# Features at two distances from the weights, modulo 256 bytes, in a decoder trunk of fp32r products

## The chip, the core and the metric

The kernel runs on one core of a Trainium2 chip. The metric is the device time of the whole program in microseconds, the lower the better. An engine has its own instruction stream: TensorE (PE, with its weight loads shown as PEld), VectorE (DVE), ScalarE (ACT), GpSimd (POOL) and SyncE (SP), which issues the transfers. [...]

## The reference: two macaron layers

The program computes two layers on x of 512 positions by 1024 channels. Each layer is a feed-forward, a mixer and a second feed-forward:

```python
def swiglu(h, w_gate, w_up, w_down):
    return (jax.nn.silu(h @ w_gate) * (h @ w_up)) @ w_down
...
    for l in range(DEPTH):
        x = x + 0.5 * swiglu(rms_norm(x, ffn1_norm[l]), ffn1_w_gate[l], ffn1_w_up[l], ffn1_w_down[l])

        h = rms_norm(x, mix_norm[l])
        a, g, q, k, v = jnp.split(h @ w_in[l], splits, axis=-1)
...
        x = x + jnp.concatenate([conv_out, diff_out], axis=-1) @ w_out[l]

        x = x + 0.5 * swiglu(rms_norm(x, ffn2_norm[l]), ffn2_w_gate[l], ffn2_w_up[l], ffn2_w_down[l])
```

The feed-forward is 2816 wide, 22 tiles of 128. The mixer has a causal convolution and a differential attention side by side.

## The kernel before

**Layout.** Channels lie on the 128 partitions, positions along the free axis, so x is 8 tiles of 128x512 and all of it stays in the on-chip memory. The weights stream in by SyncE's transfers into `wraw`.

**Products by two parts.** Every fp32 operand is split into a high part in fp32r and the rest, also in fp32r: ScalarE copies to `whi`, VectorE subtracts to `wlo` (`parts_of`, lines 105 to 112; `Unit.hi` and `Unit.lo`, lines 387 to 396). A product is then three matmuls, high by high, high weights by low features, low weights by high features (`mm3`, lines 144 to 150; `Unit.product`, lines 405 to 411). The first operand of a matmul is loaded into the array (the weights, 128x128, recorded as a weight load of its own), the second moves through it (the features, 512 or 256 columns). In the projections to q, k and v (lines 988 to 990 and 1018 to 1020) the roles are swapped: a 128x128 piece of features is loaded and 512 columns of weights move.

**A feed-forward** (`ffn`, from line 800) does its 22 tiles in three parts (`PARTS`, line 45). The first 5 are plain: full-width products of 512 columns on `acts` (the scaled x, lines 146, 149, 150), then 480 matmuls in all four feed-forwards for their down product (`ps_d`, on the features `hh` and `hl`). The other 17 tiles, in groups of 8 and 9, go by a Strassen-like scheme of seven products on halves: one `Unit` is one tile's gate and up (`GateUp`) or two output tiles' down products (`Down`), and each of its seven products is four steps of three matmuls 256 columns wide, all at line 409: 84 matmuls. `Unit.body` writes the order of a unit out by hand: while PE does one unit, ScalarE and VectorE split the next one's weights, and GpSimd adds its sums of weights (lines 381 to 385). A feed-forward has 17 `GateUp` and 8 `Down`, in this order: one unit of the first group, its other seven, one of the second, the four `Down` of the first, the other eight, the four `Down` of the second. The ninth tile of the second group is done in full-width products on `sixes` (`plain`, line 640).

**Where the operands of line 409 come from.** `Halves` (line 322) makes what `GateUp` reads: the normalised features, written back over `acts` by `settle` (b11, b21, t1, b22 in `get`), and their sums in `sixes` (t2, t3, t4). `Gated` (line 691) makes what `Down` reads: the gated features in `hh` and `hl` and their sums in tiles named `hs`, for which `part` (line 707) finds twelve places a group, most in the feed-forward's own memory, some in tiles that are free at that time (`rb`, `ssum`, `sq`, `ones_r`, the last tile of `acts`).

**Memory.** Tiles come from pools that are laid one behind the other in the order of lines 79 to 84: const, small, rp (the raw weights), act (x, acts, rb), wp (whi, wlo and their short kinds), tmp (ssum, two sq). A pool opened later (the feed-forward's, the mixer's) lies behind them. Inside a pool tiles lie in the order of their first use. The class `Room` (line 224) makes the feed-forward's memory of a few large blocks: `sixes` of 12 tiles, h0 of 10 and h1 of 12, h3 and h2 of two each, every one `LINE` = 32 elements (128 bytes) longer than its content, which starts `OFF` = 16 elements (64 bytes) in. `acts` has the same form. A block that serves a second purpose is renewed as a whole (`renew`).

Of the kernel before, what the change touches and what calls it, by code (L numbers as in the profile page):

```python
# [18 lines left out]
P = 128  # L19
# [28 lines left out]

SPACE = 408
GAP = 6  # L50
OFF = 16
LINE = 32
SQ = 16
WRAW = 1040
# [19 lines left out]
def trunk(ctx: ExitStack, tc: tile.TileContext, xt, par, lamv, relb, onehot,  # L74
# [24 lines left out]
    def ring(tag, n=1024):  # L99
        if tag == "wraw":  # L100
            return rp.tile([P, WRAW], F32, tag=tag, name=tag, bufs=RING[tag])
        dt = F32 if "raw" in tag else F32R
        return wp.tile([P, n], dt, tag=tag, name=tag, bufs=RING[tag])

# [119 lines left out]
    class Room:  # L224

        def __init__(self, pool):
            self.tile = pool.tile
            self.sixes = self.tile([P, 12 * SEQ + LINE], F32R, tag="sixes", name="sixes")
            names = [[f"{t}{n}" for n in ns for t in ("hh", "hl")] for ns in (range(5), (5, 6), (7,), (8,))]
            names[1] += [f"s{n}" for n in range(5)] + ["ht"]  # L230
            self.where = {name: (k, n) for k, group in enumerate(names) for n, name in enumerate(group)}
            self.blocks = [self.block("h0", 10), self.block("h1", 12, F32), None, None]

        def block(self, tag, n, dtype=F32R):
            return self.tile([P, n * SEQ + LINE], dtype, tag=tag, name=tag)[:, OFF : OFF + n * SEQ]

        def renew(self, k, dtype):
            self.blocks[k] = self.block(f"h{k}", (10, 12, 2, 2)[k], dtype)

        def feat(self, tag):  # L240
            k, n = self.where[tag]
            return self.blocks[k][:, n * SEQ : (n + (3 if tag == "ht" else 1)) * SEQ]

    class Prep:


        def __init__(self, l, gain):
            self.l, self.gain = l, gain
            self.hi, self.lo = acth, actl
            self.s = tmp.tile([P, SEQ], F32, tag="ssum", name="ssum", bufs=1)  # L250

# [9 lines left out]
        def squares(self, k, pin=False):  # L261
            sq = self.s if k == 0 else tmp.tile([P, SEQ + SQ], F32, tag="sq", name="sq")[:, GAP : GAP + SEQ]
# [59 lines left out]
    class Halves:  # L322
# [3 lines left out]

        def __init__(self, fp, pr, r):
            t = fp.sixes[:, OFF : OFF + 12 * SEQ].rearrange("p (i n j c) -> p i n j c", i=2, n=3, j=KT // 2)
            self.th, self.tl = t[:, 0], t[:, 1]

            self.whole = []
            a, b = slice(0, HS), slice(HS, SEQ)
            ht = fp.blocks[1][:, 8 * SEQ : 11 * SEQ].rearrange("p (i n c) -> p i n c", i=2, n=3)
            for j in range(KT // 2):
                for k in (j, j + KT // 2):
                    h = fp.blocks[1][:, len(self.whole) * SEQ : (len(self.whole) + 1) * SEQ]
                    V.scalar_tensor_tensor(h, x[:, k, :], col(pr.l, pr.gain, k), r, op0=ALU.mult, op1=ALU.mult)
                    self.whole.append((k, h))
# [9 lines left out]
        def settle(self):  # L348

            for k, h in self.whole:  # L350
                S.activation(acth[:, k, :], h, AF.Copy)
                V.tensor_tensor(actl[:, k, :], h, f32(acth[:, k, :]), op=ALU.subtract)

        def get(self, name):
            if name[0] == "t" and name != "t1":
                n = int(name[1]) - 2
                return lambda j: (self.th[:, n, j, :], self.tl[:, n, j, :])
            k0, c = {"b11": (0, 0), "t1": (0, HS), "b21": (KT // 2, 0), "b22": (KT // 2, HS)}[name]
            return lambda j: (acth[:, k0 + j, c : c + HS], actl[:, k0 + j, c : c + HS])

# [197 lines left out]
    class Down(Unit):  # L558
# [121 lines left out]
        def rest(self):  # L680
# [8 lines left out]
            self.after(B)  # L689

    class Gated:

        def __init__(self, fp, pairs, many, ahead=False):
            self.fp, self.pairs, self.many, self.ahead = fp, pairs, many, ahead
# [5 lines left out]
        def hold(self, n):  # L700
            if self.ahead and not n:
                return const.tile([P, P + SPACE], F32, tag="ones_r", name="hold")[:, :SEQ]
            if n == (2 if self.ahead else 0):
                self.fp.renew(2 if self.ahead else 3, F32)
            return self.fp.feat(("hh", "hl")[n // 2 % 2] + ("7" if self.ahead else "8"))

        def part(self):

            if not self.slots:
                ht, off = self.fp.feat("ht"), slice(OFF, OFF + SEQ)  # L710
                self.slots = [lambda n=n: ht[:, n * SEQ : (n + 1) * SEQ] for n in range(3)]
                self.slots.append(lambda: act.tile([P, SEQ + LINE], F32R, tag="rb", name="hs")[:, off])
                self.slots += [lambda n=n: self.fp.feat(f"s{n}") for n in range(5)]
                if not self.ahead:
                    self.slots.append(lambda: tmp.tile([P, SEQ], F32R, tag="ssum", name="hs", bufs=1))
                    self.slots += [lambda: tmp.tile([P, SEQ + SQ], F32R, tag="sq", name="hs")[:, off]] * 2
                if self.ahead:
                    self.slots += [
                        lambda: acth[:, KT - 1, :], lambda: actl[:, KT - 1, :],
                        lambda: const.tile([P, P + SPACE], F32R, tag="ones_r", name="hs")[:, off],  # L720
                    ]
            return self.slots.pop(0)()

        def part_ninth(self):

            self.nine = hi, lo = [self.fp.sixes[:, 2 * n * SEQ : 2 * (n + 1) * SEQ] for n in range(2)]
# [30 lines left out]
        def part_hi(self, n, us):  # L757
            if self.spot(n) > 6:
                self.fp.renew(self.spot(n) - 5, F32R)
            hi, lo = (self.fp.feat(f"{t}{self.spot(n)}") for t in ("hh", "hl"))  # L760
            pinned(S.activation(hi, us, AF.Copy))
# [37 lines left out]

    def ffn(pr, gu, dn, after, turn, lead=None, aside=None):  # L800
        with tc.tile_pool(name="ffn", bufs=1) as pool:
            fp = Room(pool)
            r = halves = None
            held, h = [], Gated(fp, 0, PLAIN)
            for m in range(PLAIN):
# [29 lines left out]
                if not halves:  # L835
                    halves = Halves(fp, pr, r)
# [17 lines left out]
            for m0, many, pairs in PARTS[1:]:  # L854
                end = m0 + many == FT
                h = Gated(fp, pairs, many, end)
                gates = [GateUp(fp, halves, gu[m0 + n, 0], gu[m0 + n, 1], n, h) for n in range(many)]
# [392 lines left out]
    for l in range(DEPTH):  # L1250
# [11 lines left out]

        turn = ffn(pr, gu1[l], dn1[l], then(l, "mix_norm"), 2, *((lead, aside) if l == 0 else ()))
        mixer(l, nxt["p"], then(l, "ffn2_norm"), turn)
        ffn(nxt["p"], gu2[l], dn2[l], then(l + 1, "ffn1_norm") if l + 1 < DEPTH else last, 0)
        pr = nxt["p"]
# [74 lines left out]
```

## Time and profile before

| | us |
|---|---|
| median of 3 runs | 1747.37 |
| lowest and highest run | 1746.35, 1750.32 |
| the profiled execution | 1747.69 |
| its span, from the first instruction to the last | 1745.9 |
| PE busy | 1736.4 |
| DVE busy | 1399.3 |
| ACT busy | 1000.0 |
| POOL busy | 891.5 |

A row of the page's groups reads: line, engine, operation, written tile and read tiles, shapes, count, busy us, mean ns of one, and after a second bar the idle time of the engine before them. A matmul's own duration there includes the time in which the next one already runs; from one start to the next is what it costs. A row of the timeline reads: start us, length us, engine, line, operation, tiles, shapes and count. A row of windows reads: the stretch, its length, and for each engine busy us and the count of instructions, then the granted clock, the share of the DMA engines and GB/s.

### The profile page before, as it was taken

The page shows a single profiled execution, that of the slowest core. Times are in us where ns is not written, and L with a number is a line of the kernel's source. Part 1 is how long each engine was busy: PE and PEld are TensorE (multiplying, and loading weights), DVE is VectorE, ACT ScalarE, POOL GpSimd, SP SyncE. Part 2 cuts the span into 40 slices and gives each one's busy share as a digit, 9 for nine tenths or more (in the row PEclk, how much of TensorE's full clock was granted, in tenths as well). Part 3 has the DMA queues.
Part 4 walks back from the last instruction along what each step waited for, and adds up shares of the span by engine and source line. Part 5 has one row for each costly group of instructions (what it writes and reads, how often), then busy time and mean ns, then how long its engine had stood idle before and what let it go on. Part 6 is the DMA issues. An engine that isn't in the chain of part 4 may idle for free.

```text
span 1745.9 us, 30798 instructions
## 1 busy us (share of the span) xinstructions
PE 1736.4 (99%) x12013; PEld 1601.2 (92%) x12013; DVE 1399.3 (80%) x2049; ACT 1000.0 (57%) x1607; POOL 891.5 (51%) x664
## 2 busy tenths in 40 slices
PE   9999999999999999999999999999999999999998
PEld 7899999988788899999988999999887888999998
DVE  6978888868867868888968788888788588788886
ACT  6456566655844456556634665665558354565663
POOL 3165655468753145555503555554787432455552
PEclk9999999999999999999999999999999999999999
DMA  6233333423022233333432333334230232333332
GB/s 229 91 121 100 110 108 103 165 73 104 29 85 85 74 108 102 108 106 109 133 97 73 100 107 110 114 104 145 84 109 25 73 107 75 99 108 109 110 97 86
DMA packets 82932, 177.91 MB, mean 102 GB/s; under 512 B 8952, under 2 KB 30727, under 8 KB 82785
## 3 DMA queue, kind: packets, MB, share of 16 engines
q1 hardware_dynamic: 81184, 174.10, 31.3%
q8 instruction: 94, 1.54, 0.4%
q0 software_dynamic: 1312, 1.67, 0.3%
q14 instruction: 54, 0.43, 0.1%
q10 hardware_dynamic: 288, 0.16, 0.0%
HBM read 173.79 MB, written 3.42 MB: 101 GB/s over the span
## 4 chain that ended last, share of the span: by engine, by line
PE 97%; DVE 2%; ACT 1%; issue 0%; DMA 0%; POOL 0%; DVEq 0%; ACTq 0%; SPq 0%
PE ps_pair L409 55%; PE ps_pair L146 6%; PE ps_pair L149 6%; PE ps_pair L150 6%; PE ps_d L146 2%; PE ps_d L149 2%; PE ps_d L150 2%; PE ps_sc L1112 2%; PE ps_pair L989 2%; PE ps_out L149 2%; PE ps_pair L990 2%; PE ps_pair L988 2%; PE ps_out L150 2%; PE ps_out L146 2%; PE ps_o L1142 1%; PE ps_v L1018 1%
## 5 line engine op out<-in xcount | busy, mean ns | idle before, releaser
L396 DVE TENSOR_TENSOR wlo<-wraw,whi 128x1024 fp32r<-128x1024 f32 (+1 forms) x400 | 497.7, 1252 | 136.5 <-ACT whi L392 133.3
L392 ACT ACTIVATE whi<-wraw 128x1024 fp32r<-128x1024 f32 (+1 forms) x400 | 377.5, 953 | 255.9 <-PE ps_pair L409 116.9
L382 POOL TENSOR_TENSOR wraw<-wraw 128x512 f32<-128x512 f32 x100 | 120.8, 1208 | 585.7 <-DVE wlo L396 281.9
L409 PE MATMUL ps_pair<-acts,whi 128*128 128x256 f32 x2240 | 403.2, 280 | 0.0
L409 PEld LDWEIGHTS ps_pair<-acts,whi 128*128 128x128 f32 x2240 | 342.1, 188 | 0.3
L409 PE MATMUL ps_pair<-acts,wlo 128*128 128x256 f32 x1120 | 312.8, 279 | 0.0
L409 PE MATMUL ps_pair<-sixes,whi 128*128 128x256 f32 x1632 | 291.0, 279 | 0.0
L409 PE MATMUL ps_pair<-h,whi 128*128 128x256 f32 x1536 | 282.0, 280 | 0.3 <-ACT keep L459 0.3
L409 PEld LDWEIGHTS ps_pair<-sixes,whi 128*128 128x128 f32 x1632 | 248.0, 188 | 0.0
L409 PEld LDWEIGHTS ps_pair<-h,whi 128*128 128x128 f32 x1536 | 238.5, 188 | 3.4 <-ACT keep L459 1.0
L409 PE MATMUL ps_pair<-sixes,wlo 128*128 128x256 f32 x816 | 227.7, 279 | 0.0
L109 ACT ACTIVATE whi<-wraw 128x1024 fp32r<-128x1024 f32 (+3 forms) x124 | 123.5, 1002 | 154.4 <-PE ps_pair L149 83.2
L409 PEld LDWEIGHTS ps_pair<-acts,wlo 128*128 128x128 f32 x1120 | 210.2, 188 | 0.0
L409 PE MATMUL ps_pair<-h,wlo 128*128 128x256 f32 x736 | 205.6, 279 | 0.0
L149 PE MATMUL ps_pair<-acts,whi 128*128 128x512 f32 x448 | 175.4, 392 | 0.0
L150 PE MATMUL ps_pair<-acts,wlo 128*128 128x512 f32 x448 | 175.0, 392 | 0.0
L146 PE MATMUL ps_pair<-acts,whi 128*128 128x512 f32 x448 | 174.3, 395 | 0.0
L385 POOL TENSOR_TENSOR wraw<-wraw 128x512 f32<-128x512 f32 x100 | 152.9, 1529 | 7.8
L384 POOL TENSOR_TENSOR wraw<-wraw 128x512 f32<-128x512 f32 x100 | 151.5, 1515 | 7.8
L409 PEld LDWEIGHTS ps_pair<-sixes,wlo 128*128 128x128 f32 x816 | 155.0, 190 | 0.0
L383 POOL TENSOR_TENSOR wraw<-wraw 128x512 f32<-128x512 f32 x100 | 147.1, 1471 | 7.6
L409 PEld LDWEIGHTS ps_pair<-h,wlo 128*128 128x128 f32 x736 | 138.8, 189 | 0.0
(218 smaller groups left out, 3422.5 us busy)
## 6 DMA issues: line engine op xcount, KB each, us to landing
wraw<-in_gu SPq DMA_DIRECT2D x172, 512.0 KB, 3.9
wraw<-in_wqkv SPq DMA_DIRECT2D x24, 512.0 KB, 3.8
wraw<-in_wag SPq DMA_DIRECT2D x16, 512.0 KB, 3.7
wraw<-in_wout SPq DMA_DIRECT2D x16, 512.0 KB, 3.7
wraw<-in_dn SPq DMA_DIRECT2D x60, 128.0 KB, 3.1
wraw<-in_dn SPq DMA_DIRECT2D x20, 384.0 KB, 3.2
wraw<-in_dn SPq DMA_DIRECT2D x28, 256.0 KB, 3.0
wraw<-in_dn SPq DMA_DIRECT2D x20, 320.0 KB, 3.3
```

Source lines behind the costliest of these rows:

```text
L109: S.activation(hi, raw, AF.Copy)
L146: first = T.matmul(ps, wh, xh, start=start, stop=False)
L149: T.matmul(ps, wh, xl, start=False, stop=False)
L150: T.matmul(ps, wl, xh, start=False, stop=stop)
L382: G.tensor_tensor(d, g1, u1, op=ALU.add)
L383: G.tensor_tensor(u1, u2, u1, op=ALU.add)
L384: G.tensor_tensor(m0, g1, u1, op=ALU.add)
L385: G.tensor_tensor(m1, g2, m0, op=ALU.add)
L392: pinned(S.activation(hi, raw, AF.Copy), pin)
L396: pinned(V.tensor_tensor(out=lo, in0=raw, in1=f32(hi), op=ALU.subtract), pin)
L409: mm = T.matmul(ps, l, r, start=first and i == n == 0, stop=False, skip_group_check=True)
L988: T.matmul(ps[n], xh[:, t], wh, start=k == 0, stop=False)
```

## The change

No instruction is added or taken away; the tiles lie at other addresses. The weights' pool comes behind tmp. The two halves of `acts` are padded by `MOST` = 64 elements each, and `split(by)` gives views of them that start `by` elements in: full-width products read `split(0)`, while `settle` writes and `GateUp` reads `split(48)`, 192 bytes further on. The feed-forward's pool begins with a tile `off` of 48 elements, so that all its tiles lie 192 bytes further. `Room` goes: each feature is a tile of its own name again, without padding. `ssum` gets 48 elements of padding, `sq` 8 in place of 16, `ones_r` 392 in place of 408, `rb` none.

```diff
-SPACE = 408
+SPACE = 392
 GAP = 6
-OFF = 16
-LINE = 32
-SQ = 16
+NEAR, FAR = 48, 0
+MOST, SHIFT = 64, (48, 48, 48, 48)
...
+    tmp = ctx.enter_context(tc.tile_pool(name="tmp", bufs=2))
     wp = ctx.enter_context(tc.tile_pool(name="wp", bufs=1))
-    tmp = ctx.enter_context(tc.tile_pool(name="tmp", bufs=2))
...
-    acts = act.tile([P, 2 * KT * SEQ + LINE], F32R, tag="acts", name="acts")[:, OFF : OFF + 2 * KT * SEQ]
-    acts = acts.rearrange("p (n k c) -> p n k c", n=2, k=KT)
-    acth, actl = acts[:, 0], acts[:, 1]
+    acts = act.tile([P, 2, KT * SEQ + MOST], F32R, tag="acts", name="acts")
+
+    def split(by):
+        return [acts[:, n, by : by + KT * SEQ].rearrange("p (k c) -> p k c", k=KT) for n in range(2)]
+
+    acth, actl = split(0)
...
-        r = act.tile([P, SEQ + LINE], F32, tag=tag, name=tag)[:, :SEQ]
+        r = act.tile([P, SEQ], F32, tag=tag, name=tag)
...
-            self.s = tmp.tile([P, SEQ], F32, tag="ssum", name="ssum", bufs=1)
+            self.s = tmp.tile([P, SEQ + NEAR], F32, tag="ssum", name="ssum", bufs=1)[:, :SEQ]
...
-        def __init__(self, fp, pr, r):
-            t = fp.sixes[:, OFF : OFF + 12 * SEQ].rearrange("p (i n j c) -> p i n j c", i=2, n=3, j=KT // 2)
-            self.th, self.tl = t[:, 0], t[:, 1]
+        def __init__(self, fp, pr, r, by):
+            self.hi, self.lo = split(by)
+            self.th = fp.tile([P, 3, KT // 2, HS], F32R, tag="th", name="th")
+            self.tl = fp.tile([P, 3, KT // 2, HS], F32R, tag="tl", name="tl")
...
-                S.activation(acth[:, k, :], h, AF.Copy)
-                V.tensor_tensor(actl[:, k, :], h, f32(acth[:, k, :]), op=ALU.subtract)
+                S.activation(self.hi[:, k, :], h, AF.Copy)
+                V.tensor_tensor(self.lo[:, k, :], h, f32(self.hi[:, k, :]), op=ALU.subtract)
...
         def plain(self, n, us):
-            hi, lo = self.fp.feat(f"hh{n}"), self.fp.feat(f"hl{n}")
+            hi = self.fp.tile([P, SEQ], F32R, tag=f"hh{n}", name="hh")
+            lo = self.fp.tile([P, SEQ], F32R, tag=f"hl{n}", name="hl")
...
-    def ffn(pr, gu, dn, after, turn, lead=None, aside=None):
-        with tc.tile_pool(name="ffn", bufs=1) as pool:
-            fp = Room(pool)
+    def ffn(pr, gu, dn, after, turn, by, lead=None, aside=None):
+        with tc.tile_pool(name="ffn", bufs=1) as fp:
+            if by:
+                fp.tile([P, by], F32, tag="off", name="off")
...
             halves.settle()
-            fp.renew(1, F32R)
```

The last part of `Gated` changes in the same manner: `hold`, `part`, `part_ninth` and `part_hi` take tiles by their names.

More of the change, by code (lines that the diff above doesn't have):

```diff
@@ L102, in ring @@
         dt = F32 if "raw" in tag else F32R
-        return wp.tile([P, n], dt, tag=tag, name=tag, bufs=RING[tag])
+        more = FAR if "raw" in tag else 0
+        return wp.tile([P, n + more], dt, tag=tag, name=tag, bufs=RING[tag])[:, :n]
     def parts_of(raw, hi, lo, eng=None, first=False, pin=False):
@@ L219, in spread @@
                 tc.keep_in_program_order(mm)
-        r = act.tile([P, SEQ + LINE], F32, tag=tag, name=tag)[:, :SEQ]
+        r = act.tile([P, SEQ], F32, tag=tag, name=tag)
         S.activation(r, ps, AF.Copy)
         return r
[L224 to L242, printed above, removed]
     class Prep:
@@ L261, in squares @@
         def squares(self, k, pin=False):
-            sq = self.s if k == 0 else tmp.tile([P, SEQ + SQ], F32, tag="sq", name="sq")[:, GAP : GAP + SEQ]
+            sq = self.s if k == 0 else tmp.tile([P, SEQ + 8], F32, tag="sq", name="sq")[:, GAP : GAP + SEQ]
             square = S.activation(sq, x[:, k, :], AF.Square)
@@ L322, in trunk @@
     class Halves:
-        def __init__(self, fp, pr, r):
-            t = fp.sixes[:, OFF : OFF + 12 * SEQ].rearrange("p (i n j c) -> p i n j c", i=2, n=3, j=KT // 2)
-            self.th, self.tl = t[:, 0], t[:, 1]
+        def __init__(self, fp, pr, r, by):
+            self.hi, self.lo = split(by)
+            self.th = fp.tile([P, 3, KT // 2, HS], F32R, tag="th", name="th")
+            self.tl = fp.tile([P, 3, KT // 2, HS], F32R, tag="tl", name="tl")
             self.whole = []
+            free = [f"{t}{n}" for t in ("hh", "hl") for n in range(5, 9)]
             a, b = slice(0, HS), slice(HS, SEQ)
-            ht = fp.blocks[1][:, 8 * SEQ : 11 * SEQ].rearrange("p (i n c) -> p i n c", i=2, n=3)
+            ht = fp.tile([P, 2, 3, HS], F32, tag="ht", name="ht")
             for j in range(KT // 2):
                 for k in (j, j + KT // 2):
-                    h = fp.blocks[1][:, len(self.whole) * SEQ : (len(self.whole) + 1) * SEQ]
+                    h = fp.tile([P, SEQ], F32, tag=free.pop(), name="hn")
                     V.scalar_tensor_tensor(h, x[:, k, :], col(pr.l, pr.gain, k), r, op0=ALU.mult, op1=ALU.mult)
@@ L689, in rest, with one_tile, __init__ @@
             self.after(B)
+    def one_tile(pool, tag, dtype, name, bufs=None):
+        return pool.tile([P, SEQ], dtype, tag=tag, name=name, **({"bufs": bufs} if bufs else {}))
     class Gated:
-        def __init__(self, fp, pairs, many, ahead=False):
+        def __init__(self, fp, pairs, many, by, ahead=False):
+            self.by = by
             self.fp, self.pairs, self.many, self.ahead = fp, pairs, many, ahead
@@ L702, in hold @@
                 return const.tile([P, P + SPACE], F32, tag="ones_r", name="hold")[:, :SEQ]
-            if n == (2 if self.ahead else 0):
-                self.fp.renew(2 if self.ahead else 3, F32)
-            return self.fp.feat(("hh", "hl")[n // 2 % 2] + ("7" if self.ahead else "8"))
+            return one_tile(self.fp, ("hh", "hl")[n // 2 % 2] + ("7" if self.ahead else "8"), F32, "hold")
         def part(self):
             if not self.slots:
[L710 to L713, printed above, removed]
+                ht = self.fp.tile([P, 3, SEQ], F32R, tag="ht", name="hs")
+                self.slots = [lambda n=n: ht[:, n] for n in range(3)]
+                tags = [(act, "rb", None)] + [(self.fp, f"s{n}", None) for n in range(5)]
                 if not self.ahead:
-                    self.slots.append(lambda: tmp.tile([P, SEQ], F32R, tag="ssum", name="hs", bufs=1))
-                    self.slots += [lambda: tmp.tile([P, SEQ + SQ], F32R, tag="sq", name="hs")[:, off]] * 2
+                    tags += [(tmp, "ssum", 1), (tmp, "sq", None), (tmp, "sq", None)]
+                self.slots += [
+                    lambda pool=pool, tag=tag, bufs=bufs: one_tile(pool, tag, F32R, "hs", bufs)
+                    for pool, tag, bufs in tags
+                ]
                 if self.ahead:
                     self.slots += [
-                        lambda: acth[:, KT - 1, :], lambda: actl[:, KT - 1, :],
-                        lambda: const.tile([P, P + SPACE], F32R, tag="ones_r", name="hs")[:, off],
+                        *(lambda t=t: t[:, KT - 1, :] for t in split(self.by)),
+                        lambda: const.tile([P, P + SPACE], F32R, tag="ones_r", name="hs")[:, :SEQ],
                     ]
@@ L724, in part_ninth @@
         def part_ninth(self):
-            self.nine = hi, lo = [self.fp.sixes[:, 2 * n * SEQ : 2 * (n + 1) * SEQ] for n in range(2)]
+            th = self.fp.tile([P, 6, SEQ], F32R, tag="th", name="nine")
+            self.nine = hi, lo = [th[:, 2 * n : 2 * n + 2, :].rearrange("p n c -> p (n c)") for n in range(2)]
             S.activation(hi, self.ninth, AF.Copy)
@@ L757, in part_hi @@
         def part_hi(self, n, us):
-            if self.spot(n) > 6:
-                self.fp.renew(self.spot(n) - 5, F32R)
-            hi, lo = (self.fp.feat(f"{t}{self.spot(n)}") for t in ("hh", "hl"))
+            hi = one_tile(self.fp, f"hh{self.spot(n)}", F32R, "hh")
+            lo = one_tile(self.fp, f"hl{self.spot(n)}", F32R, "hl")
             pinned(S.activation(hi, us, AF.Copy))
@@ L835, in ffn @@
                 if not halves:
[L836 removed]
+                    halves = Halves(fp, pr, r, by)
             turn += PLAIN
             halves.settle()
[L839 removed]
             blocks = [divmod(kk, HALF) for kk in range(PLAIN)]
@@ L855, in ffn @@
                 end = m0 + many == FT
-                h = Gated(fp, pairs, many, end)
+                h = Gated(fp, pairs, many, by, end)
                 gates = [GateUp(fp, halves, gu[m0 + n, 0], gu[m0 + n, 1], n, h) for n in range(many)]
@@ L1261, in last @@
             nc.sync.dma_start(out[m], x[:, m, :])
-        turn = ffn(pr, gu1[l], dn1[l], then(l, "mix_norm"), 2, *((lead, aside) if l == 0 else ()))
+        turn = ffn(pr, gu1[l], dn1[l], then(l, "mix_norm"), 2, SHIFT[2 * l], *((lead, aside) if l == 0 else ()))
         mixer(l, nxt["p"], then(l, "ffn2_norm"), turn)
-        ffn(nxt["p"], gu2[l], dn2[l], then(l + 1, "ffn1_norm") if l + 1 < DEPTH else last, 0)
+        ffn(nxt["p"], gu2[l], dn2[l], then(l + 1, "ffn1_norm") if l + 1 < DEPTH else last, 0, SHIFT[2 * l + 1])
         pr = nxt["p"]
```

4 lines of the change are left out of this document (2 added, 2 removed).

## The prediction

> **What bounds the kernel now.** I read the page first: span, engines, the chain of waits.
>
> ```profile
> span 1745.9 us, 30798 instructions
> PE 1736.4 (99%) x12013; PEld 1601.2 (92%) x12013; DVE 1399.3 (80%) x2049; ACT 1000.0 (57%) x1607; POOL 891.5 (51%) x664
> ...
> PE 97%; DVE 2%; ACT 1%; issue 0%; DMA 0%; POOL 0%; DVEq 0%; ACTq 0%; SPq 0%
> ```
>
> TensorE holds 97% of the chain and lacks only 1745.9 − 1736.4 = 9.5 us of being busy throughout. So time can only come from the pace of one matmul after another. The groups of PE, shapes apart, say how many there are of each kind (columns: line, operation, tiles, shapes, count, busy us, mean ns):
>
> ```profile
> L409 PE MATMUL ps_pair<-acts,whi 128*128 128x256 f32 x2240 | 403.2, 280 | 0.0
> L409 PE MATMUL ps_pair<-acts,wlo 128*128 128x256 f32 x1120 | 312.8, 279 | 0.0
> L409 PE MATMUL ps_pair<-sixes,whi 128*128 128x256 f32 x1632 | 291.0, 279 | 0.0
> L409 PE MATMUL ps_pair<-h,whi 128*128 128x256 f32 x1536 | 282.0, 280 | 0.3 <-ACT keep L459 0.3
> L409 PE MATMUL ps_pair<-sixes,wlo 128*128 128x256 f32 x816 | 227.7, 279 | 0.0
> L409 PE MATMUL ps_pair<-h,wlo 128*128 128x256 f32 x736 | 205.6, 279 | 0.0
> ...
> L149 PE MATMUL ps_pair<-acts,whi 128*128 128x512 f32 x448 | 175.4, 392 | 0.0
> ...
> L149 PE MATMUL ps_d<-h,whi 128*128 128x512 f32 x160 | 62.2, 392 | 0.0
> ...
> L989 PE MATMUL ps_pair<-wlo,acts 128*128 128x512 f32 x128 | 50.6, 398 | 0.0
> ...
> L409 PE MATMUL ps_pair<-hs,whi 128*128 128x256 f32 x192 | 43.3, 280 | 0.0
> L149 PE MATMUL ps_out<-acts,whi 128*128 128x256 f32 x128 | 35.9, 281 | 0.0
> L409 PE MATMUL ps_pair<-hs,wlo 128*128 128x256 f32 x128 | 35.8, 280 | 0.0
> ...
> L1018 PE MATMUL ps_v<-whi,acts 128*128 128x512 f32 x64 | 25.8, 408 | 0.0
> L149 PE MATMUL ps_out<-acts,whi 128*128 128x512 f32 x64 | 25.9, 404 | 0.0
> ```
>
> The half-width products of line 409 are 2240+1120+1632+1536+816+736+192+128 = 8400. The full-width ones come in threes of lines, each line with the count shown: 3×448 = 1344 first products, 3×160 = 480 plain downs, 3×(128+64) = 576 with the projections' weights as moving operand, 3×64 = 192 of the output projection, which also has 3×128 = 384 half-width ones. The mean of one overlaps its neighbours; the pace has to be read from starts. The long pieces of the chain (start us, length us, count) give it:
>
> ```profile
> 90.83 212.00 PE ps_pair L409 x1812
> ...
> 622.32 120.04 PE ps_pair L409 x1019
> 742.55 80.69 PE ps_pair L409 x683
> ...
> 959.07 210.31 PE ps_pair L409 x1812
> ...
> 1488.57 207.49 PE ps_pair L409 x1764
> ```
>
> Together 830.53 us for 7090 matmuls: 117.14 ns each, so the 8400 cost 984.0 us. But the pieces differ, 116.1 ns in the fourth and 118.1 in the third, for the same work. Windows of PE show it inside one feed-forward (busy us, matmuls):
>
> ```profile
> 100.00:180.00 80.00, 80.00 (x692) 1.00 0.33 106
> 220.00:300.00 80.00, 80.00 (x682) 1.00 0.32 100
> ```
>
> PE is full in both, at clock 1.00, and yet ten matmuls apart. The timeline of PE tells what differs; a row of "wlo" is each third matmul:
>
> ```profile
> 94.75 0.28 PE L409 MATMUL ps_pair<-acts,wlo 128*128 128x256 f32 x1
> ...
> 97.58 0.28 PE L409 MATMUL ps_pair<-acts,wlo 128*128 128x256 f32 x1
> ...
> 101.05 0.28 PE L409 MATMUL ps_pair<-sixes,wlo 128*128 128x256 f32 x1
> ...
> 103.09 0.28 PE L409 MATMUL ps_pair<-sixes,wlo 128*128 128x256 f32 x1
> ...
> 632.29 0.28 PE L409 MATMUL ps_pair<-sixes,wlo 128*128 128x256 f32 x1
> ...
> 634.41 0.28 PE L409 MATMUL ps_pair<-sixes,wlo 128*128 128x256 f32 x1
> ```
>
> On acts 24 starts take 2.83 us, 117.9 ns. On sixes 18 take 2.04 us, **113.3 ns**, in the first feed-forward, and 2.12 us, **117.8 ns**, in the second. There are two paces, 4.5 ns apart, and nothing between lasts.
>
> Which operand lies where follows from the tile sizes. From acts to the first weight tile are 32,896 + 2,176 bytes, 137×256; acts starts 64 bytes in, so its features are read 64 above the weights' phase. The ring of weights is 43,008 bytes, 168×256; ssum and the two sq behind it are 2,048 + 4,224, an odd number of half lines, so sixes lies at 128 + 64 = 192. Its size adds half a line again: h0 is at 64, h1 at 192. So phase 192 knows the fast pace and phase 64 is nearly always at the slow one. Nearly: one stretch on acts, as a piece of the chain,
>
> ```profile
> 1088.92 4.09 PE ps_pair L409 x36
> ```
>
> has 113.6 ns. The phase is thus not the whole cause; the sequence before has a say, and a pace once taken is kept while the phase stays.
>
> **The change, part by part.** Full-width first. Two rows each of the chain, on acts (phase 64, each third start) and in the projections (weights moving, features stationary, so −64, which is 192; L989 is each third too):
>
> ```profile
> 42.08 0.23 PE ps_pair L146
> ...
> 60.62 0.23 PE ps_pair L146
> ```
>
> ```profile
> 377.91 0.24 PE ps_pair L989
> ...
> 397.51 0.24 PE ps_pair L989
> ```
>
> 81 starts in 18.54 us are 228.9 ns; 84 in 19.60 us are 233.3 ns. The step is 4.4 ns again.
>
> Where the change puts things: acts becomes 2×16,640 bytes, rb 2,048, ssum 2,240, two sq 4,160, now ahead of the weights; the sum from acts to the weights is 41,728, 163×256, so unshifted features are at phase 0. Half-width products read copies written 192 bytes further, and the feed-forward's pool, which still lies behind the 43,008 bytes of weights, opens with an unused tile of 192 bytes, behind which every tile is a multiple of 256. So all features there are at 192, the plain downs' too. Exceptions are few: of a group's twelve hs tiles, rb, ssum and the second sq fall elsewhere in the first group, rb and ones_r in the second.
>
> (1) *Half-width products, 64 or 192 to 192.* A gate/up unit has 7×12 = 84 matmuls; 17 units in each of four feed-forwards make 5712, the eight Downs 2688. Gate/up units alternate 48 matmuls on acts with 36 on sixes now; afterwards nothing in them changes phase, so a pace would stay from start to end. Which one is set on entry. The nearest entry is a full-width product ahead of half-width ones at 192:
>
> ```profile
> 310.07 0.85 PE L409 MATMUL ps_d<-h,sixes 128*128 128x512 f32 x3
> ...
> 310.99 0.28 PE L409 MATMUL ps_pair<-h,wlo 128*128 128x256 f32 x1
> ...
> 311.67 0.28 PE L409 MATMUL ps_pair<-h,wlo 128*128 128x256 f32 x1
> ```
>
> Six starts in 0.68 us: 113.3 ns, fast at once. After the change the plain downs, full-width at 192, precede the units in the same way. I take the fast pace for all gate/up units, 5712×113.3 = 647.2 us, and for the Downs, whose hs exceptions disturb it, the middle of the paces, 115.55: 310.6 us. Together 957.8 against 984.0: **−26.2 us**. Ends: all fast, 951.7 (−32.3); Downs all slow, 963.8 (−20.2).
>
> (2) *Full-width at phase 0*, a phase that no long stretch shows. Bounds: one step below the better pace, 228.9 − 4.4 = 224.5, and the worse pace seen, 233.3. I take 228.9, between the two. First products and output projection, 1536: 0 us, ends −6.8 and +6.8. Projections, 576 from 233.3: −2.5 us, ends −5.1 and 0.
>
> (3) *Plain downs, 64 to 192*: 480 × 4.4 = +2.1 us.
>
> (4) *Half-width output products, 384, 64 to 0*: taken at the same pace, 0; one step either way is 1.7 us.
>
> (5) *Instructions.* None is added on any engine, no DMA either. The blocks of the Room class become tiles by name, so a renewal waits for one feature's readers and not a block's; PE's 9.5 us idle is all that could win, and I take 0. Settling writes 192 bytes into the next tile's old place, so it waits for that tile's first products as well; the 120 plain downs of a feed-forward, 120×228.9 ns = 27 us, stand between those and the first half-width product and hide it. The raw weights keep their distance to whi modulo 256 (both shift by 64). And VectorE:
>
> ```profile
> 960.00:1060.00 100.00, 100.00 (x864) 100.00 (x863) 83.38 (x111) 65.54 (x103) 55.25 (x40) 1.00 0.33 101
> ```
>
> 83.38 us for 864 matmuls is 96.5 ns each, under 113.3, so it does not become the bound.
>
> Sum: −26.2 − 2.5 + 2.1 = −26.6 us. The profiled execution took 1747.69 us, 1.79 more than its span and 0.3 above the median of 1747.37; 1747.69 − 26.6 = **1721.1 us**. Own range: 1747.69 − 32.3 − 11.9 + 2.1 − 1.7 = 1704 to 1747.69 − 20.2 + 6.8 + 2.1 + 1.7 = 1738.
>
> **Rivals.** *A, the fast pace is lost at the first Downs* of each feed-forward and not found again. Nine units are fast (3024×113.3), 5376 matmuls slow at 117.8: 975.9 us, −8.1; with −2.5 and +2.1, **1739.2**. For it: the windows above, 692 and then 682, on either side of the Downs. Against: the entry at 310.07, which is fast in the midst of Downs.
>
> *B, slower: the slow pattern holds at 192*, as at 632.29, in all 8400 matmuls, and phase 0 is as bad for full-width products as 192. 8400×117.8 = 989.5, +5.5; first and output products +6.8, projections 0, plain downs +2.1: +14.4, **1762.1**. With full-width products so dear, the half-width ones must win 8.9 us, a mean of 116.1 ns; it decides below a fast share of (117.8 − 116.1)/4.5 = 38%. For it: of the pieces of the chain three run near 118 ns, and the sixes of those feed-forwards at 117.8. Against: these come out of phase 64 each time, which the change takes away.
>
> *C, the phase is not what sets the pace*, and it does not do what it says: two paces at one phase (632.29, 1088.92) speak for that, and the time stays, **1747.7**. [...]
>
> **How the numbers follow.** Forecast 0.53, A 0.18, B 0.20, C 0.09. About 0.2% (3.5 us) is what a measurement of this kernel can tell from no change. Faster: forecast and A, less 0.01, 0.70; within: C and that 0.01, 0.10; slower: B, 0.20. Time 1721; range 1705 to 1750, which takes in A and C and leaves B out.
>
> **What would show it.** Right: chain pieces of line 409 at 113 to 114 ns a matmul in the gate/up units, five windows of 80 us with over 700 matmuls each; first products at 228.9 or less for each start; plain downs at 233.3. Wrong: pieces at 117.8, which is B, or fast up to about 180 us and slow after, which is A; first products over 233.3; or PE idle well above 9.5 us, released by VectorE or ScalarE, which would put the loss in the new tiles' waits.

## The result, and the profile after

The kernel with the change takes **1727.34 us**, the median of 4 runs (1726.90 to 1729.03), beside 1748.84 for the kernel before in the same session. The ratio is 0.988, with a 95% interval of 0.9863 to 0.9897. The profiled execution took 1727.72 us. Its page:

```profile
span 1725.9 us, 30801 instructions
...
PE 1711.5 (99%) x12013; PEld 1577.4 (91%) x12013; DVE 1401.0 (81%) x2049; ACT 1000.2 (58%) x1607; POOL 899.8 (52%) x664
...
PE 89%; DVE 6%; ACT 2%; issue 2%; POOL 1%; DMA 1%; DVEq 0%; SPq 0%; ACTq 0%; POOLq 0%
```

The span fell by 20.0 us, PE's busy time by 24.9. PE is now idle for 1725.9 − 1711.5 = 14.4 us, 4.9 more than before, and VectorE's share of the chain went from 2% to 6%: matmuls became faster, and a part of that went into new waits. The trace holds three instructions more than before (30801, 30798), none of them on PE, VectorE, ScalarE or GpSimd, whose counts are the same.

The Strassen products are at line 394 now. Their long pieces in the chain (start us, length us, count):

```profile
91.78 160.43 PE ps_pair L394 x1391
...
617.49 116.14 PE ps_pair L394 x1019
734.63 42.52 PE ps_pair L394 x371
...
947.79 115.97 PE ps_pair L394 x1019
...
1472.05 107.88 PE ps_pair L394 x948
```

The second, fourth and fifth are 113.8 to 114.0 ns a matmul; the same 1019 took 120.04 us before. The first is 115.3 ns. Of five windows of 80 us in the units, four hold over 700 matmuls (704 to 707) and one does not. Here are the worst and the best (busy us, matmuls, clock):

```profile
100.00:180.00 80.00, 80.00 (x690) 1.00 0.35 109
...
960.00:1040.00 80.00, 80.00 (x707) 1.00 0.34 106
```

For the full-width products, first two rows of PE's timeline on `acts`, each line being every third start:

```profile
50.02 0.39 PE L146 MATMUL ps_pair<-acts,whi 128*128 128x512 f32 x1
...
52.74 0.39 PE L146 MATMUL ps_pair<-acts,whi 128*128 128x512 f32 x1
```

and from the chain, a stretch of the plain downs and one of the projections:

```profile
68.45 0.23 PE ps_d L150
...
77.55 0.23 PE ps_d L150
```

```profile
379.07 0.23 PE ps_pair L978
...
386.55 0.23 PE ps_pair L978
```

At phase 0, 12 starts take 2.72 us and 33 take 7.48 us: **226.7 ns** both times, 2.2 less than the 228.9 of before. At 192, 39 starts take 9.10 us: 233.3 ns. The half-width products of the output projection are at phase 0 too:

```profile
515.82 0.28 PE L150 MATMUL ps_out<-acts,wlo 128*128 128x256 f32 x1
...
524.82 0.28 PE L150 MATMUL ps_out<-acts,wlo 128*128 128x256 f32 x1
```

75 starts in 9.00 us are 120.0 ns, 2 ns more than before. So phase 0 is the best found for 512 columns and among the worst for 256.

The new waits, by what PE waited for (us in total, times, longest):

```profile
PE ps_pair L394 <- ACT keep L444: 4.0, 4, 1.4
...
PE ps_pair L394 <- DVE nine L718: 0.5, 3, 0.2
```

Before, the same wait for `keep` had 0.3 us once. Three of the four lie in the last of the first group's four Downs, the fourth in the third Down of the second group. Here is the one in the second feed-forward, engine by engine (VectorE, GpSimd, ScalarE, TensorE):

```profile
729.33 0.68 DVE L381 TENSOR_TENSOR wlo<-wraw,whi 128x512 fp32r<-128x512 f32 x1
```

```profile
730.08 1.10 POOL L367 TENSOR_TENSOR wraw<-wraw 128x512 f32<-128x512 f32 x1 [2.10 <-DVE wlo L381]
731.26 1.95 POOL L368 TENSOR_TENSOR wraw<-wraw 128x512 f32<-128x512 f32 x1
```

```profile
733.25 1.06 ACT L377 ACTIVATE whi<-wraw 128x1024 fp32r<-128x1024 f32 x1 [3.96 <-POOL wraw L368]
734.21 0.37 ACT L444 ACTIVATE keep<-ps_pair 128x256 f32<-128x256 f32 x1
```

```profile
733.45 0.28 PE L394 MATMUL ps_pair<-hs,wlo 128*128 128x256 f32 x1
734.63 0.51 PE L394 MATMUL ps_pair<-hs,whi 128*128 128x256 f32 x2 [0.91 <-ACT keep L444]
```

GpSimd's first sum of the unit stood 2.10 us, until VectorE had read the one buffer `wraw2` (the 512-wide `wlo`); ScalarE's next `whi` stood 3.96 us until the sums were done, the `keep` copy stands behind `whi` in ScalarE's stream, and PE stood 0.91 us until `keep` had read `ps_pair`. PE starts 1.18 us after the matmul before. No feature's tile holds this chain up; that PE simply arrives earlier is what the experiments below try.

All starts of PE, each to the next, summed by class (matmuls; a start more than 139 ns after the one before counts as a wait, and since the start behind a wait is late too, by some 110 ns, the 24 are 13 places):

```
class                          before     after     difference
half-width, pace               983.4      959.1      -24.3
half-width, waits (3 -> 24)      0.5        6.2       +5.7
first products                 310.1      308.4       -1.7
plain downs                    109.9      112.0       +2.1
projections                    136.5      132.9       -3.6
output, full width              45.6       45.4       -0.2
output, half width              45.3       46.2       +0.9
ninth tiles                     24.0       25.2       +1.2
                                               sum   -19.9 us
```

The wait for `keep` in the second group's Downs is in the last row, since it follows a product of the ninth tile: 1.41 us from start to start against 0.66 before, 0.75 of the 1.2. The rest of that row is the pace of its 512-column products, 233.9 ns against 230.6, and slightly longer waits for `nine`.

Why the first piece is slower shows at 131 us, in PE's timeline:

```profile
129.94 0.28 PE L394 MATMUL ps_pair<-th,wlo 128*128 128x256 f32 x1
...
130.96 0.28 PE L394 MATMUL ps_pair<-th,wlo 128*128 128x256 f32 x1
131.15 0.39 PE L394 MATMUL ps_pair<-th,whi 128*128 128x256 f32 x1
...
131.84 0.28 PE L394 MATMUL ps_pair<-th,wlo 128*128 128x256 f32 x1
...
135.73 0.28 PE L394 MATMUL ps_pair<-acts,wlo 128*128 128x256 f32 x1
```

Nine starts in 1.02 us, 113.3 ns; then a wait of 190 ns where 113 are due; then 33 starts in 3.89 us, **117.9 ns**, which lasts to about 185 us. The addresses are the same before and after the wait. The other three feed-forwards have the wait at this place as well (216 ns at 657 us, 193 at 987, 204 at 1511) and go on at 113.3. A second such stretch runs from 1647 to 1685 us, at 117.8 ns behind a wait of 396.

### The profile page after: what moved, and what is told of

Read it like the earlier page. It is cut to its first block, busy times and chain, and to the rows that moved or that the text cites. A ratio compares the mean times of both kernels' runs of the same rounds, so it can differ in the third digit from the quotient of the medians.

```text
span 1725.9 us, 30801 instructions
## 1 busy us (share of the span) xinstructions
PE 1711.5 (99%) x12013; PEld 1577.4 (91%) x12013; DVE 1401.0 (81%) x2049; ACT 1000.2 (58%) x1607; POOL 899.8 (52%) x664
## 4 chain that ended last, share of the span: by engine, by line
PE 89%; DVE 6%; ACT 2%; issue 2%; POOL 1%; DMA 1%; DVEq 0%; SPq 0%; ACTq 0%; POOLq 0%
PE ps_pair L394 47%; PE ps_pair L146 6%; PE ps_pair L150 6%; PE ps_pair L149 6%; DVE wlo L381 2%; PE ps_d L150 2%; PE ps_d L149 2%; PE ps_d L146 2%; PE ps_sc L1102 2%; PE ps_out L149 2%; PE ps_out L146 2%; PE ps_out L150 2%; PE ps_pair L978 2%; PE ps_pair L979 2%; PE ps_pair L980 2%
## 5 line engine op out<-in xcount | busy, mean ns | idle before, releaser
L367 POOL TENSOR_TENSOR wraw<-wraw 128x512 f32<-128x512 f32 x100 | 115.9, 1159 | 563.9 <-DVE wlo L381 262.7
L394 PE MATMUL ps_pair<-acts,whi 128*128 128x256 f32 x2240 | 390.8, 277 | 0.0
L394 PE MATMUL ps_pair<-th,whi 128*128 128x256 f32 x816 | 226.6, 278 | 0.5
L394 PE MATMUL ps_pair<-th,wlo 128*128 128x256 f32 x816 | 225.7, 277 | 0.0
L394 PE MATMUL ps_pair<-tl,whi 128*128 128x256 f32 x816 | 225.7, 277 | 0.0
L368 POOL TENSOR_TENSOR wraw<-wraw 128x512 f32<-128x512 f32 x100 | 161.5, 1615 | 7.6
L370 POOL TENSOR_TENSOR wraw<-wraw 128x512 f32<-128x512 f32 x100 | 159.1, 1591 | 7.8
L394 PEld LDWEIGHTS ps_pair<-th,whi 128*128 128x128 f32 x816 | 153.2, 188 | 1.7 <-ACT keep L444 1.3
L394 PEld LDWEIGHTS ps_pair<-th,wlo 128*128 128x128 f32 x816 | 153.6, 188 | 0.0
L394 PEld LDWEIGHTS ps_pair<-tl,whi 128*128 128x128 f32 x816 | 153.2, 188 | 0.0
L369 POOL TENSOR_TENSOR wraw<-wraw 128x512 f32<-128x512 f32 x100 | 143.5, 1435 | 7.8
L394 PE MATMUL ps_pair<-hh,whi 128*128 128x256 f32 x512 | 141.9, 277 | 0.0
L394 PE MATMUL ps_pair<-hl,whi 128*128 128x256 f32 x512 | 141.7, 277 | 0.0
```

What stands on the lines that cost most here:

```text
L367: G.tensor_tensor(d, g1, u1, op=ALU.add)
L368: G.tensor_tensor(u1, u2, u1, op=ALU.add)
L369: G.tensor_tensor(m0, g1, u1, op=ALU.add)
L370: G.tensor_tensor(m1, g2, m0, op=ALU.add)
L394: mm = T.matmul(ps, l, r, start=first and i == n == 0, stop=False, skip_group_check=True)
```

## The experiments

My theory was that the distance from the weights modulo 256 sets the pace, that PE's pace alone brings the waits, and that the tiles by name do nothing. The rivals: the gain comes from the tiles, or the waits do, or the phase is only a bystander of how a stretch begins.

**No shift (all0).** All features at phase 0, everything else as in the change:

```diff
-MOST, SHIFT = 64, (48, 48, 48, 48)
+MOST, SHIFT = 64, (0, 0, 0, 0)
```

> All features of the feed-forwards at the weights' phase, 0, in place of 192; the tiles by name stay. Theory, the phase sets the pace: the 8400 half-width matmuls go at the 120.0 ns that the output projection's half-width products show at phase 0 after the change (46.2 us for 384), 1008 us against 959 without waits; the plain downs win 480 x 6.6 ns = 3.2 us; about 1767 us. If the new waits of PE (24 in line 394, 6 us) come only from PE being faster, they fall under 1 us here. Rival, the gain of the change comes from the tiles by name and not from the phase: about 1725 us, and the waits stay.

1767.08 us in one run. The chain's pieces:

```profile
90.54 220.59 PE ps_pair L394 x1838
...
626.96 220.59 PE ps_pair L394 x1838
```

120.0 ns in both, with no second pace for the units and not one wait inside the half-width products, 1006.9 us in all. With the same tiles, the same order and other addresses the kernel is 40 us slower than the change. So the gain is the phase, and at this pace none of the change's 24 waits (6.2 us) is there.

**Each phase (map1, map2).** A different shift in each feed-forward: 32, 64, 96, 128 bytes, then 160, 224, 64, 128.

```diff
-MOST, SHIFT = 64, (48, 48, 48, 48)
+MOST, SHIFT = 64, (8, 16, 24, 32)
...
+MOST, SHIFT = 64, (40, 56, 16, 32)
```

> The four feed-forwards at 32, 64, 96 and 128 bytes in place of 192, each a map of its own phase for half-width products and for 120 full-width plain downs. Theory, phase in steps of 64: half-width at 64 keeps to 117.8 ns (before: 78 of 78 entries from a fast stretch fell to it), 128 lies between 113.3 and 122, 32 goes as 0 (120.0) or as 64 and 96 as 64 or 128, whichever step it falls into; full-width at 64 228.9. Rival, tiles by name: all four at 113 to 114 ns.

> The four feed-forwards at 160, 224, 64 and 128 bytes. Theory, phase: 64 and 128 repeat the paces of the other map within 0.5 ns though they stand in the third and fourth feed-forward; 224 lies between 113.3 (192) and 120.0 (0), 160 between 128 and 192. Rival, the pace hangs on the place in the program: 64 and 128 differ from the other map by more than 2 ns.

1755.54 and 1752.34 us, one run each. The pieces of the first, in the order of the phases 32, 64, 96, 128 (64 in two pieces):

```profile
92.08 212.45 PE ps_pair L394 x1812
621.88 120.17 PE ps_pair L394 x1020
742.07 80.73 PE ps_pair L394 x683
959.04 220.58 PE ps_pair L394 x1838
1494.46 214.94 PE ps_pair L394 x1812
```

They are 117.2, 117.8 and 118.2, 120.0 and 118.6 ns. From these and the starts of the other runs, the steady paces in ns:

```
phase         0      32      64      96     128     160     192     224
256 cols  120.0   116.7   113.3   120.0   118.7   118.7   113.3   118.4
                 or 117.8 or 117.8                      or 117.8
512 cols  226.7   233.3   228.9   233.3   233.3   234.3   233.3   233.3
```

128 came out alike in both kernels to 0.1 ns; 64 did so but for its third feed-forward in the second kernel, which ran five units after its Downs at 113.3. The place in the program falls as a rival. But the expected steps of 64 bytes did not hold: 96 has 120.0 ns, the pace of neither 64 nor 128, and with 512 columns 32 has neither that of 0 nor that of 64. Of the eight only 64 and 192 showed 113.3 ns, and 512 columns were fastest at 0, by 2.2 ns.

**The blocks of before at the addresses of the change (room).** Class `Room` again, without its padding, behind the same 192 bytes (`BY` = 48 elements):

```diff
-OFF = 16
-LINE = 32
+OFF = 0
+LINE = 0
...
+            self.tile([P, BY], F32, tag="off", name="off")
             self.sixes = self.tile([P, 12 * SEQ + LINE], F32R, tag="sixes", name="sixes")
```

> The addresses of the change with the blocks of before: features in the few large blocks of the Room class again, all phases as after the change (0 and 192). Theory, the gain is the phase and the waits come from PE's speed: as after the change, 1727 us, and 4 to 7 us of waits in the half-width products. Rival, the tiles by name brought the new waits: these fall to about 1 us and the time to 1722. Rival, the tiles by name brought the gain: back towards 1748.

1726.42 us (1725.12 to 1726.68, 4 runs), ratio 0.9873 [0.9856, 0.9889]. Half-width products 965.1 us against 965.3 for the change, with 24 waits of 5.5 us against 24 of 6.2. The tiles by name bring neither the gain nor the waits. The stretches at 117.8 lie elsewhere, in the second and third feed-forward's first group.

**Full-width at 64 (full64).** Half-width products stay at 192:

```diff
-    acth, actl = split(0)
+    acth, actl = split(16)
```

> The change with its full-width part alone undone: the unshifted features of acts 64 bytes above the weights, half-width ones still at 192. Theory: first and output products 1536 x (228.9 - 226.7) = +3.4 us, the projections, whose role is turned, at 192 and 233.3: 576 x 6.6 = +3.8 us, the half-width output products 384 x (117.8 - 120.0) = -0.8 us; +6.4 us, ratio to before 0.992. Rival, full-width products do not care: 1727 us, 0.988.

1741.92 us (1740.86 to 1744.70, 10 runs), ratio 0.9969 [0.996, 0.9979], 8 more than expected. The full-width products were as expected. The projections tell most, for here the weights move, and they lie where they lay in the change:

```profile
374.55 0.23 PE ps_pair L978
...
394.15 0.23 PE ps_pair L978
```

84 starts in 19.60 us are 233.3 ns against 226.7 in the change, though only the loaded features lie elsewhere. In the other products a shift of the features that move, alone, changed the pace (120.0 ns in all0 against 113.3). So in these runs neither address set it by itself; it went with how the two lie to each other. The units were not as expected, in all four feed-forwards. In the second:

```profile
621.14 119.45 PE ps_pair L394 x1019
```

This piece is 117.2 ns; its first nine units ran at 117.8 and the half-width products came to 973.8 us, 8.5 more than in the change. They are entered from the same plain downs at 192 as there; only what ran before those differs, 64 in place of 0. So here the pattern was not set by the entry alone: the stretch at 192 handed on what it had found.

**Attention's output products at 192 (out192, out192b).** The half-width ones, 384:

```diff
+            ah, al = split(48)
...
-                S.activation(ch[:, CT:, tq], pt, AF.Copy, scale=gsub[l])
+                S.activation(ah[:, CT:, tq], pt, AF.Copy, scale=gsub[l])
```

> The change, and the attention's half of the output projection's features 192 bytes above the weights too: its 384 half-width products go from 120.0 ns (phase 0) to 113.3: -2.6 us, 1725 us. If only the class of line 394 has the two paces, nothing moves.

1725.12 us in one run. PE's timeline of the first kernel, to compare with the 9.00 us above:

```profile
516.03 0.28 PE L150 MATMUL ps_out<-acts,wlo 128*128 128x256 f32 x1
...
524.87 0.28 PE L150 MATMUL ps_out<-acts,wlo 128*128 128x256 f32 x1
```

75 starts in 8.84 us are 117.9 ns: the slow pattern of 192, after full-width products at 0. The 384 win 0.8 us and not 2.5. So the same kernel was timed again:

> The kernel with the attention half of the output projection at 192, now in five rounds beside the one above. 384 half-width products at 113.3 instead of 119.9 ns are worth 2.5 us: 1727.3 - 2.5 = about 1725, ratio to the kernel of before about 0.987. If the single time of it was luck, it ends at the 1727 of the change.

1728.35 us (1726.19 to 1729.13, 4 runs), ratio 0.9881 [0.9866, 0.9896], not to be told from the change. The profiled executions differ in the stretches at 117.8 that begin at a wait: one in the first, four in the second, 300 to 470 matmuls by 4.5 ns or 1.4 to 2.1 us each.

**Plain features at phase 0 (plain0, both).** The plain downs read their features 192 bytes lower; the second kernel has the edit above as well:

```diff
-            hi = self.fp.tile([P, SEQ], F32R, tag=f"hh{n}", name="hh")
-            lo = self.fp.tile([P, SEQ], F32R, tag=f"hl{n}", name="hl")
+            hi, lo = self.fives(n, 0)
```

> The change, and the plain features at the weights' phase: the five pairs of feature tiles in one block that plain products read from its start and half-width ones 192 bytes further on. 480 plain downs go from 233.3 to 226.7 ns: -3.2 us, 1724 us. But the half-width units are then entered from full-width products at 0 and not at 192: if the pace is set on entry, some feed-forwards may start at 117.8 ns, each up to 750 x 4.5 = 3.4 us for its first nine units.

> Both edits, output projection and plain downs: -2.6 - 3.2 us, 1721.5 us, ratio to before 0.985, if the paces add up. If the entry from phase 0 makes a feed-forward slow, 1725 or more.

1732.46 us in one run, and 1733.01 (1729.56 to 1735.18, 4 runs), ratio 0.991 [0.9896, 0.9925]: slower than the change, though the downs ran at 226.7. The first nine units are at 117.8 in all four feed-forwards, in both kernels. The second, in PE's timeline, right behind its last plain down:

```profile
90.45 0.39 PE L150 MATMUL ps_d<-five,wlo 128*128 128x512 f32 x1
...
90.92 0.28 PE L394 MATMUL ps_pair<-acts,wlo 128*128 128x256 f32 x1
...
93.04 0.28 PE L394 MATMUL ps_pair<-th,wlo 128*128 128x256 f32 x1
```

18 starts in 2.12 us, 117.8 ns from the first on.

**One plain tile of five back at 192 (mix).** An edit of the second kernel of these two:

```diff
-            hi, lo = self.fives(n, 0)
+            hi, lo = self.fives(n, self.by if n == PLAIN - 1 else 0)
```

> Edit to the last kernel: of the five plain feature tiles of an FFN, the first four are read at phase 0 and the fifth at 192, so each output tile of the plain downs ends with three full-width products at 192 and the gate/up units are again entered from 192, after a stretch of only three products (0.7 us). If the pattern of the half-width products is set by the last few full-width products ahead of them, the first nine units of each FFN run at 113.3 ns again: about 1733.0 - 4 x 756 x 4.5 ns = 1719.4, plus 96 x 4 / 4 x 6.6 ns = 0.6 for the tile put back, plus up to 5 us of the waits that come with the faster pace: 1720 to 1725. If it is inherited from further back (the products at phase 0 ahead of them, as the fully-64 kernel suggests), the units stay at 117.8 and the time at about 1733.5.

**1724.16 us** (1722.40 to 1725.76, 4 runs), ratio 0.9856 [0.9839, 0.9872]. The same rows, three full-width products at 192 later:

```profile
90.86 0.39 PE L150 MATMUL ps_d<-five,wlo 128*128 128x512 f32 x1
...
91.34 0.28 PE L394 MATMUL ps_pair<-acts,wlo 128*128 128x256 f32 x1
...
93.38 0.28 PE L394 MATMUL ps_pair<-th,wlo 128*128 128x256 f32 x1
```

18 starts in 2.04 us: 113.3 ns, so in all four feed-forwards (the third fell to 117.8 later, at a wait at 985 us); half-width products 965.2 us against 973.7 without this edit. Three products at 192 between phase 0 and the units were enough here to hand on the fast pattern. This version has the lowest median of all; its runs lie below the change's, by about the 3.3 us that its edits are worth (384 downs by 6.6 ns, and 0.8), while the intervals of the two ratios overlap.

**A second wraw2 for a fifth of the raw ring (mix_wraw2).** An edit of mix:

```diff
-    RING = {"wraw": 5, "whi": 4, "wlo": 4, "wraw2": 1, "whi2": 2, "wlo2": 2}
+    RING = {"wraw": 4, "whi": 4, "wlo": 4, "wraw2": 2, "whi2": 2, "wlo2": 2}
```

> The kernel with four plain tiles at phase 0, with a second buffer for the 512-wide sum of the weights (wraw2, 1 to 2) paid for by one of the five 1024-wide raw buffers (wraw, 5 to 4). In the change, GpSimd's first sum of a unit (L367) waits until VectorE has read the single wraw2, and the chain sums, whi, keep, matmul then ends 0.2 to 1.6 us late at 24 places (6.2 us in all, 2.6 in the runs whose first units are slow). If that single buffer is what starts the chain late, L367 is no longer released by VectorE's wlo of 512, ScalarE's keep copy comes earlier, and TensorE's waits go below 2 us: 1724.2 - 4 = about 1720. If the buffer only hides another limit, the waits stay at about 6 us; and since one raw buffer fewer lets the weights' DMAs start later, they may become the releaser: then the time is 1724 or above, and a unit that waits for its weights in every round (84 matmuls, 9.5 us) would put it well above 1730.

1744.95 us (1736.12 to 1750.39, 10 runs), ratio 0.9976 [0.9958, 0.9995]. GpSimd's waits (us, times, longest) in the kernel above and in this one:

```profile
POOL wraw L367 <- DVE wlo L381: 266.7, 72, 6.7
POOL wraw L367 <- DMA wraw<-in_gu: 201.7, 11, 36.2
```

```profile
POOL wraw L367 <- DMA wraw<-in_gu: 351.8, 54, 41.0
...
POOL wraw L367 <- DVE wlo L381: 50.5, 13, 8.2
```

The single `wraw2` did release GpSimd in 72 of 100 units, and a second one takes that away in most; but with four raw buffers GpSimd's waits for the weights to land grew from 201.7 to 351.8 us and took its place, and the late starts of PE in the half-width products grew to 71 with 21.9 us. 31 of them, 3 us, are no waits but matmuls of some 213 ns, in two stretches that each begin after PE had stood for 2 us or more; two other stops of that length are not followed by one. The first, at a granted clock of 0.53 (busy us, matmuls, clock):

```profile
220.30:223.90 3.60, 3.52 (x17) 0.53 0.62 224
```

Whether a second `wraw2` beside five raw buffers would remove the 6 us stays open; it wasn't tried. So `wraw2` as the start of the late chain is not shown to the end.

This run has one thing more. The output products that stayed at 117.9 ns in out192 begin so here as well and then change, in both layers:

```profile
514.66 0.28 PE L150 MATMUL ps_out<-acts,wlo 128*128 128x256 f32 x1
...
516.43 0.28 PE L150 MATMUL ps_out<-acts,wlo 128*128 128x256 f32 x1
...
517.23 0.28 PE L150 MATMUL ps_out<-acts,wlo 128*128 128x256 f32 x1
...
520.63 0.28 PE L150 MATMUL ps_out<-acts,wlo 128*128 128x256 f32 x1
```

15 starts in 1.77 us are 118.0 ns, then 30 in 3.40 us are 113.3. Between them stand four 128-column matmuls and a start that comes 207 ns after the one before. The same break, with 203 ns, left the slow pattern in out192, out192b, both and mix. So 113.3 ns was reached there too, and slow turned into fast at a break; what decides is open.

## Why the prediction was right, and where its sum was off

**The direction and the cause** were right: 1727.34 lies in the range, and all0 and room show that the distance modulo 256 brings the gain. Rival C falls with them: two kernels with the same instructions and tiles are 40 us apart, and one shape at clock 1.00 took 120.0 ns in the one and 113.3 in the steady stretches of the other. The multiple of 256 made no difference in all0: `acts` ahead of the weights and `th` behind them lie at different multiples of 256 from them, and the 1838 matmuls on end that read both kept 120.0 ns.

**(1) Half-width, −26.2 predicted.** The pace alone won 24.3: gate/up units were fast but for two stretches that begin at a wait. The size was nearly right, in part by luck: units came to 113.9 ns and not 113.3, Downs to 114.8 and not 115.55, and the two errors, +3.4 and −2.1 us, cancel for the most part. The working was right in part: "Which one is set on entry" is only half of it. The entry from full-width products at 192 was fast because of what stood ahead of these, as full64 shows, and the pattern turned later at a wait, of 190 ns at 131 us and of 396 ns at 1647. Rival A falls: the Downs did not lose the fast pace, the units behind them were fast in each feed-forward (in the fourth until the wait at 1647 us), and in the kernels with a slow entry it was after the Downs that the fast pace came. Rival B falls for this kernel, but its pattern exists at 192: the first nine units of full64, plain0 and both, at 117.8 ns, are it.

**(5) Instructions and waits, 0 predicted.** This is the term that failed: +5.7 us. I compared VectorE's mean, 96.5 ns a matmul, with 113.3 and concluded that it does not bind. The mean was no answer to a chain: above all in the last Down of the first group, VectorE, GpSimd, ScalarE and PE stand one behind the other, and the row of 0.3 us for `keep` in the trace of before showed that the margin was already gone in the Downs. I had named PE idle above 9.5 us, released by VectorE or ScalarE, as a sign against the tiles; it came, and room shows that the tiles are not its cause, and all0 that a PE at 120 ns has none of it. Where only the first group's units were slow (full64, plain0, both) the waits were 2.6 to 3.0 us.

**(2) Full-width at 0, −2.5 predicted:** −5.5 (first −1.7, projections −3.6, output −0.2). The 226.7 ns lie inside the bounds, on the better side of the 228.9 taken. The first products won 1.7 us and not the 3.0 that 1344 × 2.2 ns would be. Their regular starts, those at the switch from tile to tile included, went from 229.1 to 227.2 ns, 2.5 us; most of the rest was lost at the program's start, to a wait that the profile of before does not have:

```profile
PE ps_pair L146 <- ACT whi L109: 0.7, 1, 0.7
```

**(3) Plain downs, +2.1 predicted:** +2.1, at 233.3. **(4) Half-width output, 0 predicted:** +0.9; the bound of one step was right and the sign was the worse one. **Not in the sum:** the ninth tiles, +1.2, of which 0.75 is again a wait for `keep`.

Together −20.0 against −26.6; the waits in the half-width products are 5.7 of the 6.6 us missed, and the terms that were off by less, up and down, make the rest. Of the signs that the prediction named, one came only in part: four of five windows have over 700 matmuls, since in the first a wait brought the slow pattern.

## What to carry to other kernels

Where PE is busy throughout, look at the spacing of starts for one shape at one clock: two values that each kept for a whole stretch, 113.3 and 117.8 ns, led here to where the two operands lie, and a shift of one of them cost nothing but bytes. Test each width by itself, since phase 0 was the fastest found for 512 columns (226.7 ns) and gave 256 columns 120.0, as slow as any. Look at the switch between two widths too: three products at 192 in between were the difference between 117.8 and 113.3 ns (both and mix). Before booking such a gain, find the rows in which PE already waits a few tenths of a us for another engine: there a part of the gain was paid back here (the waits for `keep` went from 0.3 to 4.0 us), though VectorE's mean, 96.5 ns a matmul, left room.

## What was not expected of the hardware

One shape at one phase showed two steady paces, 113.3 and 117.8 ns for 256 columns at 192, and kept the one it had for hundreds of matmuls (455 at 117.8 between 131 and 185 us); it turned from the first to the second at a wait of 190 ns at 131 us, and waits of 193 to 216 ns at the same place left it in three other feed-forwards. In mix_wraw2 it turned the other way at a break of four short matmuls, from 118.0 to 113.3 ns, in both layers. Straight from 512 columns at phase 0 to 256 at 192 gave 117.8 ns in all eight entries of plain0 and both; with three products of 512 at 192 in between it was 113.3 in all four of mix. What makes this is not shown by any run here.
